# A stated wait of 2.2 ahead of the second lane's Gram products in a hybrid RWKV-7 / S5 layer

## The chip, the cores and the metric

The kernel runs on one core of a Trainium2 chip. The time is the device time of one execution in microseconds (us); lower is better. Before the change three timed executions took 1517.97, 1521.6 and 1523.78 us, so the median is 1521.6 us. The execution that the profiler recorded took 1524.13 us by the same clock; its span, from the first to the last recorded instruction, is 1522.3 us.

The core has a matrix engine (PE, with its weight loads listed as PEld), a vector engine (DVE), an engine for activations and copies (ACT), a general engine (POOL) and a queue engine that only issues transfers (SP). Each runs its own list of instructions in order, and waits at an instruction until what it needs is there. POOL and SP issue the DMA transfers of this kernel. PE writes its results to PSUM, a memory of a few banks, from which DVE or ACT must take them before the bank can be written anew.

## The reference

One decoder layer on `x` of shape (1, 1024, 1024), in float32. Only the part around the change is given in full:

```python
h  = rms_norm(x, norm_mix_pre)
p  = h @ w_in              # RWKV columns | S5 input u | two gates
yA = rwkv7_branch(p_rwkv)  # 8 heads of 64, 1024 time steps
yB = s5_branch(u)          # diagonal complex state space, 64 states per group
m  = sigmoid(gA) * (yA @ wA) + sigmoid(gB) * (yB @ wB)
x  = x + rms_norm(m @ w_out, norm_mix_post)
x  = x + rms_norm(conv_ffn(rms_norm(x, norm_ffn_pre)), norm_ffn_post)

# inside rwkv7_branch, per head (S is 64 x 64)
S = S * w_t + (S @ a_t) b_t^T + v_t k_t^T
y_t = S @ r_t
bonus = sum(r * k * r_k, over the head) * v      # added to y
```

## The kernel before

**Matrix products.** Every large product is computed in three passes from a high and a low part of each operand (lines 180, 181, 182, on 128x512 tiles). A group of these three matmuls is called a *step* here.

**RWKV.** The recurrence is not run step by step. Time is cut into chunks of 64, and within a chunk the products of all pairs of time steps (the *Gram products*) are formed, masked, and a triangular system is inverted. The work is divided into four *pairs* i = 0..3, two groups of heads by two halves of time (512 steps each). Each pair goes through these stages:

1. the *front* (`rwkv_front`), run by two lanes u = 0 and 1, each for half of the group's heads. It ends with two sets of Gram products (line 752, 32 matmuls of 64x128 each, into two PSUM banks), their masked copy to `gr` by DVE (line 754), the transfer of the diagonal blocks to DRAM as `md` (line 760, POOL), and the *bonus sum*: one product with a block matrix of ones (line 763, into one PSUM bank), which DVE multiplies by `v` (line 764), and which is stored as `bv` (line 765).
2. the *inverse* (`rwkv_inv`): 31 steps on DVE (lines 810 and 812) on the blocks of `md`; POOL stores the result to DRAM (line 815) and loads it back into `gr` (line 822, eight transfers).
3. the *level* (`rwkv_level`): two DVE transposes of `gr` (line 835), PE products of 32x32 (line 838), ACT copies of them (line 839), PE products with these (line 840), ACT copies (line 841). It combines the 32-blocks to 64-blocks.
4. the *chain* (`rwkv_chain`, lines 870 to 913) over the chunks, and the output of the pair.

**PSUM.** The Gram products, the bonus sum and a few others draw from one tag `rp` with two banks. A set of Gram products takes both, the bonus sum takes one.

**The order.** On PE the order is that in which the program is written: the whole block runs under a manual schedule for PE. `drive()` writes it. It keeps a clock of its own, `self.now`, and a list of lanes: `chain_lane` first, then `prep_lane(0)` and `prep_lane(1)` (which run the fronts and the inverse of a pair), then a lane for a late product. Each lane is a generator. When it has written a piece it yields the PE time of the piece and a delay (or a condition) until its next piece may stand. The first lane in the list that is ready goes next; when none is ready, or too much of PE's recent time went to lanes, `background()` writes one step of the projections of the gates and of the branches, with a planned PE time of 0.68. A piece that becomes ready later therefore stands behind more such steps; the steps are the same ones, drawn from one list.

Two conditions matter here. Ahead of each set of Gram products a lane waits until `self.now >= self.masked`, and then sets `self.masked = self.now + 1.8 + T_GR` with T_GR = 2.5: the next set, of whichever lane, is not to stand before DVE has emptied the two banks. The bonus sum has no part in this: it neither waits for `masked` nor sets it.

On DVE, ACT, POOL and SP a scheduler orders the instructions by priorities and by its own estimate of when each can run. That order is fixed when the program is built.

**The tail of the program.** Behind the RWKV branch come the merge, the output projection, the norms and the feed-forward part, nearly all of it PE steps.

Of the kernel before, what the change touches and what calls it, by code (L numbers as in the profile page):

```python
# [73 lines left out]
class Kern:  # L74
# [607 lines left out]
    def rwkv_front(self, d, u, i):  # L682
# [81 lines left out]
        V.tensor_tensor(r, pb, v, ALU.mult)  # L764
        nc.gpsimd.dma_start(d["bv"][u], r)
        d["v"][u] = v
        yield 0.55, 1.5

    def rwkv_nat(self, d):
# [1329 lines left out]
T_LD, T_LT = 14.0, 3.0  # L2099
NEVA = 4  # L2100
T_KN, T_BK, T_GR, T_INV, T_LV, T_CH, T_LN, T_LF = 12.0, 10.0, 2.5, 58.0, 1.0, 0.8, 12.0, 12.0
T_X, T_GLU = 3.0, 25.0
T_N0, T_RS, T_N1, T_N2, T_N4, T_N5, T_N3 = 2.5, 4.0, 2.2, 20.0, 1.6, 24.0, 2.0
NET = 5
T_PN = 8.0
# [87 lines left out]
```

## Time and profile before

| | before |
|---|---|
| median of three timed runs | 1521.6 us (1517.97 to 1523.78) |
| the profiled execution, its own time | 1524.13 us |
| its span | 1522.3 us |
| mean granted PE clock | 0.991 of full speed |
| PE busy | 1469.8 us, 97% of the span |
| DVE busy | 1158.5 us, 76% |
| ACT busy | 726.6 us, 48% |
| POOL busy | 180.2 us, 12% |
| the RWKV stage, from the first front's Gram products to the last chain | about 290 to 720 us of the span |

The views used below: the *waits* list, for each engine and line, the time idle ahead of it and what ended the idle time; the *timeline* has one row for each run of equal instructions (start in us, duration of the run in us, engine, line, operation, output<-inputs, count, and in brackets the idle time just before and what ended it); the *windows* give, for a stretch of the span, each engine's busy time with its count of instructions, then the granted PE clock (1.00 is full speed), the busy share of the DMA engines (1.05 means that all of them were taken) and GB/s. Consecutive matmuls overlap: what counts is the distance from one start to the next, not the duration in the row. "A<-B" in brackets reads "until B of that line was done".

### The profile page before, as it was taken

The page shows a single profiled execution, that of the slowest core. Times are in us where ns is not written, and L with a number is a line of the kernel's source. Part 1 is how long each engine was busy: PE and PEld are TensorE (multiplying, and loading weights), DVE is VectorE, ACT ScalarE, POOL GpSimd, SP SyncE. Part 2 cuts the span into 40 slices and gives each one's busy share as a digit, 9 for nine tenths or more (in the row PEclk, how much of TensorE's full clock was granted, in tenths as well). Part 3 has the DMA queues.
Part 4 walks back from the last instruction along what each step waited for, and adds up shares of the span by engine and source line. Part 5 has one row for each costly group of instructions (what it writes and reads, how often), then busy time and mean ns, then how long its engine had stood idle before and what let it go on. Part 6 is the DMA issues. An engine that isn't in the chain of part 4 may idle for free.

```text
span 1522.3 us, 23902 instructions
## 1 busy us (share of the span) xinstructions
PE 1469.8 (97%) x8804; PEld 1166.1 (77%) x8804; DVE 1158.5 (76%) x2157; ACT 726.6 (48%) x1209; POOL 180.2 (12%) x340
## 2 busy tenths in 40 slices
PE   7999999999999998999999999999999999999997
PEld 5788787787677675666788778888888887888875
DVE  7989974765655594975767888888888888698767
ACT  5465444331453434556635555555555555444451
POOL 0022111124021232030110010000000000000000
PEclk9999999999999998999999999999999999999999
DMA  6455344444332446452456575233333336944712
GB/s 211 135 154 159 98 139 145 143 135 152 107 124 96 128 120 192 146 167 70 157 189 199 182 242 180 93 108 117 113 110 117 112 109 225 333 154 138 246 59 111
DMA packets 121558, 225.26 MB, mean 148 GB/s; under 512 B 31024, under 2 KB 37168, under 8 KB 121440
## 3 DMA queue, kind: packets, MB, share of 16 engines
q1 hardware_dynamic: 90576, 154.77, 32.5%
q0 software_dynamic: 21024, 64.71, 12.9%
q10 hardware_dynamic: 9840, 4.24, 1.1%
q8 instruction: 69, 1.13, 0.3%
q14 instruction: 49, 0.40, 0.1%
HBM read 164.16 MB, written 57.41 MB: 146 GB/s over the span
## 4 chain that ended last, share of the span: by engine, by line
PE 44%; DVE 4%; DMA 4%; ACT 1%; issue 1%; SPq 0%; DVEq 0%; ACTq 0%
PE d L1779 8%; PE rp L1600 5%; PE rp L1602 5%; PE rp L1601 5%; PE mm L1602 2%; PE mm L1600 2%; PE mm L1601 2%; DMA st<-in_w_down_dram 2%; PE ch L181 1%; PE mm L180 1%; PE ch L182 1%; PE mm L181 1%; PE gm L180 1%; PE ch L180 1%; PE mm L182 1%
## 5 line engine op out<-in xcount | busy, mean ns | idle before, releaser
L180 PE MATMUL gm<-hh,wh 128*128 128x512 f32 x672 | 283.1, 421 | 1.9 <-DVE ev L1057 1.9
L181 PE MATMUL gm<-hl,wh 128*128 128x512 f32 x672 | 264.9, 394 | 0.1
L182 PE MATMUL gm<-hh,wl 128*128 128x512 f32 x672 | 264.7, 394 | 0.0
L160 ACT CAST wh<-wf 128x512 fp32r<-128x512 f32 x181 | 111.9, 619 | 171.5 <-PE gm L181 88.5
L161 DVE TENSOR_TENSOR wl<-wf,wh 128x512 fp32r<-128x512 f32 x181 | 124.3, 690 | 86.5 <-ACT wh L160 84.5
L180 PEld LDWEIGHTS gm<-hh,wh 128*128 128x128 f32 x672 | 127.0, 189 | 34.3 <-issue 4.0
L182 PEld LDWEIGHTS gm<-hh,wl 128*128 128x128 f32 x672 | 127.0, 189 | 28.1
L181 PEld LDWEIGHTS gm<-hl,wh 128*128 128x128 f32 x672 | 127.4, 190 | 22.5 <-DVE hl L246 1.0
L1779 PE MATMUL d<-xh,wl 128*128 128x512 f32 x308 | 113.5, 392 | 2.1 <-DVE wl L246 2.1
L1779 PE MATMUL d<-xh,wh 128*128 128x512 f32 x308 | 113.9, 393 | 1.1 <-DVE zg L1630 1.1
L1779 PE MATMUL d<-xl,wh 128*128 128x512 f32 x308 | 113.4, 392 | 0.6 <-DVE xl L246 0.6
L1600 PE MATMUL rp<-t,h 128*128 128x512 f32 x252 | 98.3, 390 | 1.4 <-ACT p L1614 1.4
L1602 PE MATMUL rp<-t,l 128*128 128x512 f32 x252 | 98.0, 389 | 0.0
L1601 PE MATMUL rp<-t,h 128*128 128x512 f32 x252 | 98.0, 389 | 0.0
L1779 PEld LDWEIGHTS d<-xh,wl 128*128 128x128 f32 x308 | 58.1, 189 | 15.1 <-DVE wl L246 2.9
L1779 PEld LDWEIGHTS d<-xh,wh 128*128 128x128 f32 x308 | 57.8, 189 | 14.2 <-DVE zg L1630 1.5
L246 DVE TENSOR_TENSOR l<-r,h 128x1024 fp32r<-128x1024 f32 (+1 forms) x40 | 38.9, 971 | 38.9 <-ACT h L245 38.9
L1779 PEld LDWEIGHTS d<-xl,wh 128*128 128x128 f32 x308 | 58.2, 189 | 13.2 <-DVE xl L246 0.9
L245 ACT CAST h<-r 128x1024 fp32r<-128x1024 f32 (+1 forms) x40 | 33.9, 849 | 69.5 <-PE rp L1601 67.2
L1621 DVE SCALAR_TENSOR_TENSOR y<-zv,vecs,y 128x1023 f32<-128x1023 f32 (+1 forms) x42 | 53.7, 1280 | 10.2 <-ACT y L1619 10.2
L1600 PEld LDWEIGHTS rp<-t,h 128*128 128x128 f32 x252 | 47.3, 188 | 11.9 <-ACT p L1614 2.2
L1601 PEld LDWEIGHTS rp<-t,h 128*128 128x128 f32 x252 | 47.3, 188 | 9.8
(476 smaller groups left out, 3338.1 us busy)
## 6 DMA issues: line engine op xcount, KB each, us to landing
r<-in_w_up_dram SPq DMA_DIRECT2D x42, 512.0 KB, 3.5
wf<-in_w_in_dram SPq DMA_DIRECT2D x72, 256.0 KB, 3.1
st<-in_w_down_dram SPq DMA_DIRECT2D x55, 256.0 KB, 4.3
st<-ACT SPq DMA_DIRECT2D x44, 256.0 KB, 4.2
ACT<-y POOLq DMA_DIRECT2D x21, 512.0 KB, 2.9
GT<-ev POOLq DMA_DIRECT2D x32, 256.0 KB, 3.5
wf<-in_w_br_dram SPq DMA_DIRECT2D x32, 256.0 KB, 3.4
wf<-in_w_out_dram SPq DMA_DIRECT2D x32, 256.0 KB, 2.8
```

What stands on the lines that cost most here:

```text
L160: self.last_wh = nc.scalar.copy(h[:, :n], f[:, :n])
L161: low = nc.vector.tensor_tensor(l[:, :n], f[:, :n], h[:, :n].bitcast(F32), ALU.subtract)
L180: mm(ps, a, xh[k], start=a0, stop=False)
L181: mm(ps, a, xl[k], start=False, stop=False)
L182: mm(ps, b, xh[k], start=False, stop=z0)
L245: a = self.nc.scalar.copy(hi, x)
L246: self.split_ops = a, (eng or self.nc.vector).tensor_tensor(lo, x, hi.bitcast(F32), ALU.subtract)
L1600: mm(ps, wh[:, c], xh, start=first and k == 0, stop=False, skip_group_check=True)
L1601: mm(ps, wh[:, c], xl, start=False, stop=False, skip_group_check=True)
L1602: mm(ps, wl[:, c], xh, start=False, stop=k == 3, skip_group_check=True)
L1621: V.scalar_tensor_tensor(y[:, lag:], z[:, 0:1024 - lag], self.vec(nme, i), y[:, lag:], ALU.mult, ALU.add)
L1779: mm(ps, w[:, c], y[:, x], start=start and k == 0, stop=stop and k == 2, skip_group_check=True)
```

## The change

After a lane has written its bonus sum, `masked` is moved to at least `now + 2.2`. The piece that was affected by `masked` before, the next set of Gram products of either lane, now counts the bank of the bonus sum as well.

```diff
         V.tensor_tensor(r, pb, v, ALU.mult)
         nc.gpsimd.dma_start(d["bv"][u], r)
         d["v"][u] = v
+        self.masked = max(self.masked, self.now + T_PB)
         yield 0.55, 1.5
...
-T_X, T_GLU = 3.0, 25.0
+T_X, T_GLU, T_PB = 3.0, 25.0, 2.2
```

The added line shifts the numbers of all lines behind it by one: line 822 of before is 823 after, 835 is 836, 838 is 839, 839 is 840, 840 is 841, 1284 is 1285. Lines 752 to 765 keep their numbers.

No instruction is added or removed. What moves is shown at three places. First PE, in the first pair, at the end of lane 0's front; the rows are matmuls with their output tile and operands (`gm` is the bank that a projection's steps add up in, `hh`, `hl`, `wh`, `wl` the parts of the operands). Before:

```order
L180 MATMUL gm_3021<-hh_853,wh_2853 128x512
L181 MATMUL gm_3021<-hl_854,wh_2853 128x512
L182 MATMUL gm_3021<-hh_853,wl_2854 128x512
L763 MATMUL rp_3038<-ld_2628,csts 128x512
L752 MATMUL rp_3042<-ar_2745,bk_2746 64x128
L752 MATMUL rp_3043<-ar_2745,bk_2746 64x128
```

And in the changed kernel:

```order
L182 MATMUL gm_3021<-hh_853,wl_2854 128x512
L763 MATMUL rp_3038<-ld_2628,csts 128x512
L180 MATMUL gm_3021<-hh_858,wh_2859 128x512
L181 MATMUL gm_3021<-hl_859,wh_2859 128x512
L182 MATMUL gm_3021<-hh_858,wl_2860 128x512
L180 MATMUL gm_3021<-hh_863,wh_2859 128x512
L181 MATMUL gm_3021<-hl_864,wh_2859 128x512
L182 MATMUL gm_3021<-hh_863,wl_2860 128x512
L180 MATMUL gm_3021<-hh_868,wh_2859 128x512
L181 MATMUL gm_3021<-hl_869,wh_2859 128x512
L182 MATMUL gm_3021<-hh_868,wl_2860 128x512
L752 MATMUL rp_3064<-ar_2745,bk_2746 64x128
```

Lane 1's first Gram products stood directly behind lane 0's bonus sum, and now stand behind three more steps. The same is so in pair 1; in pairs 2 and 3 two or three pieces lie between, some of them products of the level (line 838) in place of steps. Everything that the lanes write behind this place stands two to six steps further back among the steps, up to the last chain; behind that the order on PE is the same as before.

Second, DVE, where pair 2 reaches its level while the front of pair 3 ends (`x` and `gr` are the tiles of the level's transpose, and the `gr` written by line 754 is that of pair 3). Before:

```order
L161 TENSOR_TENSOR wl_6352<-wf_6353,wh_6351 128x512
L835 STREAM_TRANSPOSE x_6155<-gr_4616 32x512
L754 TENSOR_TENSOR gr_5718<-rp_6132,csts 128x4x128
L835 STREAM_TRANSPOSE x_6155<-gr_4616 32x512
L754 TENSOR_TENSOR gr_5718<-rp_6133,csts 128x4x128
L161 TENSOR_TENSOR wl_6507<-wf_6508,wh_6506 128x512
L764 TENSOR_TENSOR ld_5728<-rp_6186,ld_6017 128x512
L754 TENSOR_TENSOR gr_5718<-rp_6198,csts 128x4x128
```

And in the changed kernel:

```order
L754 TENSOR_TENSOR gr_5724<-rp_6138,csts 128x4x128
L754 TENSOR_TENSOR gr_5724<-rp_6139,csts 128x4x128
L161 TENSOR_TENSOR wl_6392<-wf_6393,wh_6391 128x512
L764 TENSOR_TENSOR ld_5734<-rp_6192,ld_6023 128x512
L1285 SCALAR_TENSOR_TENSOR hl_6170<-hl_6170,gm_6178 128x512
L161 TENSOR_TENSOR wl_6557<-wf_6558,wh_6556 128x512
L836 STREAM_TRANSPOSE x_6164<-gr_4629 32x512 x2
L754 TENSOR_TENSOR gr_5724<-rp_6242,csts 128x4x128
```

The two transposes stood ahead of the bonus sum's multiplication. They now stand behind it, and behind a row that takes a finished projection from `gm_6178` and one that makes the low part of a weight. On PE the last matmul into `gm_6178` stands directly ahead of the level's first products (line 839).

Third, POOL's queue at the same place. Before:

```order
L815 DMA xd_5512<-x_5413 512x1x32 x4
L1140 DMA GT_90<-ev_6047 128x512
L696 DMA ld_6030<-RKV_102 128x512
L822 DMA gr_4616<-xd_5512 32x8x32 x8
L1140 DMA GT_89<-ev_6093 128x512
L760 DMA md_5720<-gr_5718 32x8x32 x3
L1253 DMA ev_6274<-YU_107 128x512
```

And in the changed kernel:

```order
L816 DMA xd_5540<-x_5441 512x1x32 x4
L760 DMA md_5726<-gr_5724 32x8x32
L823 DMA gr_4629<-xd_5540 32x8x32 x8
L1141 DMA GT_90<-ev_6167 128x512
L1254 DMA ev_6208<-YU_107 128x512
L1254 DMA ev_6215<-YU_108 128x512
```

The eight loads of the inverse of pair 2 into `gr`, which the transposes read, stood ahead of the first store of `md` of pair 3 and now stand behind it.

## The prediction, made before the changed kernel ran

> **What bounds the kernel now.** I read the page's busy times first, then the waits of PE, then the windows and the timeline of the RWKV stage.
>
> ```profile
> span 1522.3 us, 23902 instructions
> ...
> PE 1469.8 (97%) x8804; PEld 1166.1 (77%) x8804; DVE 1158.5 (76%) x2157; ACT 726.6 (48%) x1209; POOL 180.2 (12%) x340
> ```
>
> PE is busy for 1469.8 of 1522.3 us. Only 52.5 us are idle in the whole program, so a change that adds and removes no PE work can win a part of these and no more, apart from what it does to PE's clock. The RWKV stage holds the changed order; its window is this:
>
> ```profile
> 290.00:740.00 450.00, 432.98 (x4046) 316.92 (x4045) 291.88 (x800) 207.45 (x479) 96.40 (x177) 0.98 0.43 129
> ```
>
> PE is idle there for 450.00 - 432.98 = 17.0 us, at a mean clock of 0.98. DVE (291.88) and ACT (207.45) have room. Two lines of PE's waits lie in this stretch and are touched by the change:
>
> ```profile
> PE chk L840 <- ACT x L839: 3.8, 2, 3.4
> PE rp L752 <- DVE ld L764: 2.3, 3, 1.3
> ```
>
> The second is the wait that the change speaks of: Gram products (line 752) for the multiplication (line 764) that frees the bank of the bonus sum. The list gives 2.3 us in 3 waits. The first is the longest wait of the stage, 3.4 us in one piece, in the level of pair 2.
>
> **Term A: the waits that go.** There are four places, the end of lane 0's front in each pair. PE's timeline at the first three:
>
> ```profile
> 299.59 1.02 PE L763 MATMUL rp<-ld,csts 128*128 128x512 f32 x2
> 300.54 0.43 PE L752 MATMUL rp<-ar,bk 64*64 64x128 f32 x2
> 301.55 1.10 PE L752 MATMUL rp<-ar,bk 64*64 64x128 f32 x30 [0.58 <-DVE ld L764]
> ...
> 355.12 1.13 PE L763 MATMUL rp<-ld,csts 128*128 128x512 f32 x2
> 356.17 0.43 PE L752 MATMUL rp<-ar,bk 64*64 64x128 f32 x2
> 357.92 1.10 PE L752 MATMUL rp<-ar,bk 64*64 64x128 f32 x30 [1.32 <-DVE ld L764]
> ...
> 495.22 1.12 PE L763 MATMUL rp<-ld,csts 128*128 128x512 f32 x2
> 496.27 0.43 PE L752 MATMUL rp<-ar,bk 64*64 64x128 f32 x2
> 497.12 1.10 PE L752 MATMUL rp<-ar,bk 64*64 64x128 f32 x30 [0.42 <-DVE ld L764]
> ```
>
> Two Gram matmuls run into the free bank, and the other thirty stand until the second bank is free. And at the fourth place, with an undisturbed set of Gram products for comparison:
>
> ```profile
> 575.15 1.02 PE L763 MATMUL rp<-ld,csts 128*128 128x512 f32 x2
> 576.10 0.44 PE L838 MATMUL chb<-x,gr 32*32 32x32 f32 x16
> 576.47 1.58 PE L752 MATMUL rp<-ar,bk 64*64 64x128 f32 x32
> 577.98 0.50 PE L180 MATMUL gm<-hh,wh 128*128 128x512 f32 x1
> ...
> 581.76 1.10 PE L752 MATMUL rp<-ar,bk 64*64 64x128 f32 x32
> 582.80 0.50 PE L180 MATMUL gm<-hh,wh 128*128 128x512 f32 x1
> ```
>
> Undisturbed, 32 of them take 582.80 - 581.76 = 1.04 us to the next start, so two take 0.07. The four places lose 301.55 - 300.54 - 0.07 = 0.94, 1.75 - 0.07 = 1.68, 0.85 - 0.07 = 0.78, and 577.98 - 576.47 - 1.04 = 0.47. That is **3.9 us**. The bracketed idle times alone (the 2.3 of the list) are the lower bound, since a stopped run of matmuls also loses its overlap.
>
> Do the waits go entirely? In the new order three steps stand between. One step is the distance of two starts:
>
> ```profile
> 584.31 0.39 PE L180 MATMUL gm<-hh,wh 128*128 128x512 f32 x1
> ...
> 585.00 0.40 PE L180 MATMUL gm<-hh,wh 128*128 128x512 f32 x1
> ...
> 585.47 0.39 PE L182 MATMUL gm<-hh,wl 128*128 128x512 f32 x1
> 589.28 0.24 PE L840 MATMUL chk<-gr,x 32*32 32x32 f32 x2 [3.42 <-ACT x L839]
> ```
>
> That is 0.69 us, so Gram starts 0.95 (the bonus sum, 300.54 - 299.59) + 3 x 0.69 = 3.0 us after the bonus sum did. At place 2, the latest, DVE frees the bank here:
>
> ```profile
> 357.19 0.68 DVE L764 TENSOR_TENSOR ld<-rp,ld 128x512 f32<-128x512 f32 x1
> ```
>
> It ends at 357.87, which is 2.75 us after 355.12. The margin is 0.25 us; at places 1 and 3 Gram could go on 1.96 and 1.90 us after the bonus sum's start, so 1 us is left. I take the whole 3.9. The steps that fill the gap are drawn from the same list and would have run later, so they cost nothing in themselves, and all else that moves back among them costs nothing while its consumers have slack. In pairs 0 and 1 the inverse and the level leave it; in pair 2 they do not.
>
> **Term B: what is late next.** In pair 2 the order on DVE and POOL changes so that the level starts late. What it costs today: PE stands 3.42 us at line 840 (3.8 with the second wait of the list), because ACT puts other work ahead of the copies:
>
> ```profile
> 581.66 1.28 ACT L1254 ACT_TABLE_LOAD   x1 [6.03 <-issue]
> ...
> 587.39 0.36 ACT L839 COPY x<-chb 32x256 f32<-32x256 f32 x1
> ```
>
> and behind this stop PE runs at half clock (behind the length of a window stands PE's busy time; the granted clock is the third number from the end):
>
> ```profile
> 575.00:580.00 5.00, 4.95 (x74) 2.97 (x72) 2.67 (x4) 0.63 (x2) 3.25 (x6) 1.00 1.05 387
> ...
> 585.00:590.00 5.00, 1.16 (x8) 0.57 (x8) 4.12 (x6) 4.88 (x10) 1.17 (x3) 0.97 0.36 104
> 590.00:595.00 5.00, 5.00 (x48) 2.62 (x50) 3.45 (x6) 2.94 (x5) 3.04 (x6) 0.50 0.47 127
> 595.00:600.00 5.00, 5.00 (x37) 3.62 (x32) 0.00 (x0) 1.44 (x4) 1.94 (x4) 0.51 0.95 229
> 600.00:605.00 5.00, 4.63 (x54) 3.25 (x53) 1.86 (x4) 1.53 (x5) 0.00 (x0) 1.00 0.49 120
> ```
>
> The loss is 5 x (0.03 + 0.50 + 0.49) = 5.1 us. With the 3.8 of waiting, this place costs **8.9 us** before.
>
> In the changed kernel the first two copies stand ahead of ACT's table load, so the wait at line 840 goes. But a new one stands ahead of the level's first products (838, now 839). They need the two transposes, and these now stand on DVE behind a row (1285) that needs the projection whose last matmul stands directly ahead of 839 on PE, and behind one more row of a weight. So PE waits at least for four DVE rows in line. Each takes about 0.69 as line 764 does: 4 x 0.69 = **2.7 us** as the lower bound. The transposes also need the eight loads of line 823, and these now wait on POOL for the first `md` store:
>
> ```profile
> 565.79 4.64 POOL L822 DMA_DIRECT2D gr<-xd  x8 [1.09 <-DMA xd<-x]
> ...
> 573.42 1.17 POOL L760 DMA_DIRECT2D md<-gr  x2 [2.43 <-DVE gr L754]
> ```
>
> Before, the loads were issued from 565.79, and the first `md` store at 573.42, when Gram of lane 0 had been masked. That event keeps its distance to the bonus sum (575.15). So the loads are issued from 573.42 + 0.58 = 574.0 in steps of 4.64 / 8 = 0.58, the last at 578.06. How long they take to land, here the eight loads of before and then the weights of SP's queue at the same time:
>
> ```profile
> DMA to landing us min/median/max: 3.0/3.5/6.4
> ...
> DMA to landing us min/median/max: 3.4/5.9/8.1
> ```
>
> The last lands at 581.1 to 584.5, by the median at 581.6, and the transposes that stand behind it end 0.7 later. PE is at line 839 one step after the bonus sum, at 575.15 + 0.95 + 0.69 = 576.8. The wait is 581.6 + 0.7 - 576.8 = **5.5 us** by the median and 8.4 by the longest. I take 5.5, the value of the rows nearest to it (the same loads); the DMA share of 1.05 between 575 and 580 says that it can be more. A stop of 5.5 us is longer than the 3.42 that brought half clock before, so I put the same 5.1 us behind it. On ACT, the second pair of copies stands behind the table load and three activations; PE has some 9 us of work before it needs them (five steps, two sets of Gram products, the products of the level), at half clock twice that. I take 0 for a wait there, and 1.2 as the upper end.
>
> Term B: 5.5 + 5.1 - 8.9 = **+1.7 us**.
>
> **The sum.** -3.9 + 1.7 = -2.2 us. Against the profiled execution's own time, 1524.13, this gives 1521.9. The median of the runs is 2.5 lower than that execution (1521.6), so I predict **1519.4 us**.
>
> Bounds of the unknown: the wait at 2.7 and no loss of clock gives 2.7 - 8.9 = -6.2, with term A -10.1, so 1511.5. The wait at 8.4 with 5.1 and 1.2 behind it gives +5.8, with term A +1.9, so 1523.5.
>
> **Rivals.** *The clock comes back sooner* (faster). Half clock does not always last three windows as above. Ahead of this stretch PE had small products of the level between steps, behind it plain steps:
>
> ```profile
> 460.00:463.40 3.40, 3.40 (x10) 2.62 (x9) 3.40 (x15) 0.69 (x1) 0.55 (x1) 0.50 0.16 58
> 463.40:470.00 6.60, 6.24 (x82) 4.13 (x82) 1.46 (x7) 3.50 (x8) 0.00 (x0) 1.00 0.16 52
> ```
>
> Here it lasted 3.4 us, a loss of 1.7. With the new wait of 5.5 and one such stretch, the place costs 7.2 in place of 8.9: -1.7 - 3.9 = -5.6, so 1516.0. With a wait near 2.7, too short to lose the clock, it is the 1511.5 above. For it speaks that the place has fewer 32x32 products behind the stop than before; against it, that they are still mixed with Gram products of 64 rows, while PE was full (5.00 of 5.00) in both slow slices and it did not help.
>
> The Trainium skill, "TensorE: Matmul & The Clock Gate", section "Part 1: The HAM clock gate", states that full rate returns after at least one busy window of about 3.4 us. By this rule the sum would be the 1516.0 of this rival. The trace bears it out at 460, and not at 590 to 600, where 10 us of a full PE passed at half clock; so I weigh the rival at less than half of the forecast.
>
> *The loads of the level land late* (slower). The mechanism is the eight loads in POOL's queue behind the `md` store, in a stretch where the DMA engines are full. If the last takes 8.1 us, as the slowest weight there did, it lands at 586.2, and the wait is 586.2 + 0.7 - 576.8 = 10.1. With half clock one stretch of 3.4 us longer (1.7 more), the place costs 10.1 + 6.8 - 8.9 = +8.0, the whole +4.1, so 1525.7. The point from which it is slower than before: a wait above 8.9 + 3.9 - 5.1 = 7.7 us, that is a landing of the last load more than 5.7 us after its issue. The longest of before, 6.4, is above that; the median of 3.5 is not.
>
> *The change does not do what it says.* Gram waits at the same place for something else, for instance DVE still in the rows of the inverse at place 2, and the level comes out as before. Then the time stays at 1521.6. Against it stands the margin of 1 us at three places.
>
> **How the numbers follow.** Forecast (1511.5 to 1523.5 by its bounds, 1519.4 likeliest) 0.50; clock sooner (1511.5 to 1516.0) 0.22; loads late (1523.5 to 1527) 0.18; nothing 0.10. The range 1511 to 1527 takes all these in. A difference of 0.5%, 7.6 us, is about what a measurement of this kernel can tell from none: faster means below 1514.0, slower above 1529.2. Below 1514.0 lies about half of the second case, 0.10. Above 1529.2 only a wait much longer than the third case comes, or a second loss of clock elsewhere, 0.06. The rest is 0.84.
>
> **What would show it.** No wait of line 752 for line 764 in the waits of PE (term A). A wait of PE at line 839 for DVE's transposes (836) in the level of pair 2, of 2.7 to 8.4 us, with the clock at 0.5 behind it; the wait at line 841, 840 before, gone (term B). A clock that stays at 1.0 there, or a wait above 7.7 us, makes one of the rivals right. PE waits of over 2 us in other pairs would make the prediction wrong, since I take all other shifts as free.

## The result, and the profile after

| | before | changed |
|---|---|---|
| median of eight timed runs of each | 1522.69 us (1517.39 to 1529.79) | 1532.78 us (1530.01 to 1537.55) |
| profiled execution, its own time | 1524.13 us | 1533.01 us |
| its span | 1522.3 us | 1531.2 us |

The ratio is 1.0066, with a 95% interval of 1.0045 to 1.0086: the changed kernel is slower by some 10 us. The forecast was 1519.4 us, its range 1511 to 1527.

The page of the changed kernel, engines:

```profile
span 1531.2 us, 23895 instructions
...
PE 1473.3 (96%) x8804; PEld 1169.6 (76%) x8804; DVE 1159.7 (76%) x2157; ACT 725.9 (47%) x1209; POOL 182.0 (12%) x340
```

PE has the same 8804 matmuls. It is idle for 57.9 us against 52.5, and its busy time has grown by 3.5 us at a mean granted clock of 0.985 against 0.991. The waits of PE, and the window of the RWKV stage with its slow slices (behind the length stands PE's busy time; the clock is the third number from the end):

```profile
PE chk L889 <- DVE S L914: 8.9, 5, 5.8
PE chb L839 <- DVE x L836: 7.1, 2, 6.7
```

```profile
290.00:740.00 450.00, 427.08 (x3986) 313.80 (x3977) 288.24 (x788) 203.24 (x470) 95.85 (x175) 0.97 0.42 127
...
520.00:525.00 5.00, 3.27 (x14) 2.35 (x14) 1.88 (x4) 1.27 (x3) 0.00 (x0) 0.56 0.00 0
525.00:530.00 5.00, 5.00 (x44) 3.73 (x44) 1.27 (x5) 1.56 (x5) 0.71 (x3) 0.76 0.29 105
...
585.00:590.00 5.00, 1.70 (x18) 1.40 (x19) 1.40 (x2) 0.00 (x0) 4.64 (x10) 0.55 0.64 209
590.00:595.00 5.00, 5.00 (x69) 3.51 (x68) 1.29 (x2) 3.51 (x6) 1.06 (x2) 0.50 0.41 130
595.00:600.00 5.00, 5.00 (x57) 3.35 (x55) 2.16 (x3) 3.64 (x5) 0.56 (x1) 0.59 0.21 56
```

The wait of line 752 for line 764 is gone from the list. Two waits of 6 to 7 us have come: one at the level of pair 2 (line 839), which the prediction had, and one in the chain of pair 1 (line 889, 888 before), which it did not. Both bring half clock: the slices hold 5 x (0.44 + 0.24) = 3.4 us and 5 x (0.45 + 0.50 + 0.41) = 6.8 us of lost clock. Not all of it is a loss for PE's work. Windows of half a microsecond show that the clock halves at 520.6 and at 585.5, while PE still stands (until 521.73 and 587.88). Counted from the end of the stop, the half clock costs some 2.9 and 5.6 us.

**What the change was made for happens.** PE's timeline at the first two places:

```profile
298.08 1.02 PE L763 MATMUL rp<-ld,csts 128*128 128x512 f32 x2
...
301.10 1.10 PE L752 MATMUL rp<-ar,bk 64*64 64x128 f32 x32
...
354.81 1.12 PE L763 MATMUL rp<-ld,csts 128*128 128x512 f32 x2
...
357.95 1.10 PE L752 MATMUL rp<-ar,bk 64*64 64x128 f32 x32
```

Gram starts 3.02 and 3.14 us after the bonus sum (3.0 predicted) and runs in one piece of 32. At the third place it is 3.04.

**The new wait in chain 1.** First the changed kernel: PE at the stop, then DVE, then the queue of SP, then the same place in the kernel before (SP's queue, DVE, PE).

```profile
515.56 0.40 PE L182 MATMUL gm<-hh,wl 128*128 128x512 f32 x1
521.73 0.69 PE L889 MATMUL chk<-S,ar 64*64 64x64 f32 x8 [5.77 <-DVE S L914]
```

```profile
512.18 0.28 DVE L903 COPY UV<-chb 64x128 f32<-64x128 f32 x1 [0.85 <-PE chb L900]
520.18 1.23 DVE L718 TENSOR_TENSOR_SCAN ld<-csts,ld 128x512 f32<-128x512 f32 x1 [7.72 <-DMA ld<-TZ]
521.32 0.45 DVE L914 SCALAR_TENSOR_TENSOR S<-chb,pt,spt 128x64 f32<-128x64 f32 x2
```

```profile
510.69 0.39 SPq L696 DMA_DIRECT2D ld<-TZ  x1
```

```profile
511.21 0.38 SPq L696 DMA_DIRECT2D ld<-TZ  x1
```

```profile
518.31 1.23 DVE L718 TENSOR_TENSOR_SCAN ld<-csts,ld 128x512 f32<-128x512 f32 x1 [3.11 <-DMA ld<-TZ]
519.46 0.45 DVE L913 SCALAR_TENSOR_TENSOR S<-chb,pt,spt 128x64 f32<-128x64 f32 x2
```

```profile
519.86 0.45 PE L888 MATMUL chk<-S,ar 64*64 64x64 f32 x8 [0.60 <-DVE S L913]
```

DVE works in order. Ahead of the update of the state S in chunk 6 of chain 1 stands a scan (line 718) of pair 3's front, in both kernels. The scan needs a load into an `ld` tile, and that tile comes free only when lane 1's bonus sum of front 2 has been stored (in the changed kernel the store is issued at 507.90 and lands 2.3 us later; the load goes out at 510.69). Before, 28 matmuls of 128x512 and 80 small ones stood from that bonus sum to the last products of chunk 6, about 7.7 us of PE work at their undisturbed distances, and DVE's wait of 3.1 us cost PE 0.6. The stated wait at front 2 moves lane 1's Gram products and its bonus sum back among the steps, while the chain, first in the list of lanes, keeps its place: 22 and 64 matmuls, about 6.0 us of PE work, are left. The load also took longer: the scan starts 520.18 - 510.69 = 9.5 us after its issue, and 7.1 before. DVE now idles 7.7 us and PE 5.8. PE reaches the stop 3.3 us earlier than before (521.73 - 5.77 = 515.96 against 519.26) and the load goes out only 0.5 us earlier, so 2.8 of the 5.2 us by which PE's wait grew are the shorter distance, and 2.4 are the slower load. In the second profiles (experiment 4) the load took 8.9 us, and again 7.1 in the kernel before. Why it is slower was not tested.

**The level of pair 2.** Its loads go out late, and in this profile not for the reason that the prediction gave. POOL, DVE and PE of the changed kernel:

```profile
577.72 0.59 POOL L760 DMA_DIRECT2D md<-gr  x1 [2.58 <-DVE gr L754]
581.54 4.61 POOL L823 DMA_DIRECT2D gr<-xd  x8 [3.23 <-DMA xd<-x]
```

```profile
587.12 1.43 DVE L836 STREAM_TRANSPOSE x<-gr 32x512 f32<-32x512 f32 x2 [4.17 <-DMA gr<-xd]
```

```profile
587.88 0.31 PE L839 MATMUL chb<-x,gr 32*32 32x32 f32 x2 [6.71 <-DVE x L836]
```

The `md` store was through at 578.31; the loads stood another 3.23 us for the inverse's own store `xd` to land. The inverse itself was late. Here are the windows from its first row on DVE to its last, in the kernel before and then in the changed one (the fourth number is DVE's busy time, with its count):

```profile
527.36:559.40 32.04, 30.72 (x166) 25.64 (x165) 29.98 (x121) 15.13 (x30) 4.11 (x9) 1.00 0.34 105
```

```profile
533.17:570.72 37.55, 36.66 (x192) 30.49 (x191) 35.58 (x124) 17.39 (x32) 5.89 (x12) 1.00 0.35 116
```

It starts 5.8 us later and takes 5.5 us longer. DVE is full in both (29.98 of 32.04, 35.58 of 37.55). The inverse has 62 rows of its own in each; by the program's order 18 full-width rows of other work stand between them before, and 27 in the changed kernel. Five of the nine more belong to the last part of pair 3's front (lines 737 to 741), three make low parts (line 246) and one that of a weight (line 161). At 0.68 to 0.74 us each the nine are some 6.2 us. A third delay stands behind the inverse: from its last row to the loads it is 581.54 - 570.72 = 10.8 us, against 565.79 - 559.40 = 6.4 before, since its stores take longer to land (5.6 us from issue by the median, 2.9 before). PE itself, held in chain 1, comes to the level later too, so these delays do not add up to the wait.

In the second profile of the changed kernel (experiment 4) this wait is less than half as long, and the half clock behind it is one stretch. Its waits, POOL's rows and the windows:

```profile
PE chb L839 <- DVE x L836: 3.0, 2, 2.5
```

```profile
580.19 1.91 POOL L816 DMA_DIRECT2D xd<-x  x3 [1.58 <-issue]
586.23 0.60 POOL L760 DMA_DIRECT2D md<-gr  x1 [4.13 <-DVE gr L754]
586.87 4.61 POOL L823 DMA_DIRECT2D gr<-xd  x8
```

```profile
590.00:595.00 5.00, 2.35 (x25) 1.46 (x27) 2.36 (x4) 0.05 (x1) 3.83 (x8) 0.82 0.58 164
595.00:600.00 5.00, 5.00 (x89) 3.97 (x87) 1.29 (x2) 4.14 (x7) 2.20 (x4) 0.84 0.62 204
```

Here POOL stood 4.13 us ahead of the `md` store and issued the loads directly behind it, as the prediction had it. The inverse was late here too: its last store was issued at 581.42 and took some 4.3 us to land (the median), so that it was through only about 1 us ahead of the loads. The wait of 2.5 us in one piece is near the lower bound of 2.7 that the prediction took from four DVE rows in line. So what the level waits for, and how long, differs between two executions of the same program.

**Where the time went, by stage.** For a sum over all places, each matmul is given the distance to the next start that its shape has in the profile of before where nothing waits. Their sum is PE's work; what a stage takes beyond it is lost time (waits and half clock together). The stages are cut at equal work, with the time at which the kernel before reaches the cut. Both kernels were profiled a second time (experiment 4).

| lost time in us, up to work | 283 us | 489 | 529 | 573 | 608 | 759 | end |
|---|---|---|---|---|---|---|---|
| what stands there | ahead of the change | fronts 0 to 2 | chain 1 | front 3 | level of pair 2 | chain 2, level 3 | the rest |
| before | 18.4 | 36.1 | 10.2 | 3.8 | 15.4 | 30.8 | 21.5 |
| before, second profile | 21.0 | 36.5 | 10.3 | 3.5 | 13.9 | 32.0 | 19.6 |
| changed | 17.5 | 32.8 | 17.5 | 3.1 | 19.0 | 30.6 | 24.8 |
| changed, second profile | 21.9 | 34.7 | 16.2 | 6.4 | 17.3 | 30.8 | 22.4 |

By the means, fronts 0 to 2 give 2.6 us, chain 1 takes 6.6, front 3 takes 1.1 and the level 3.5; the stage behind it gives 0.7. The 3 us of the last column fall almost wholly where the order of all engines is the same in both kernels (from 777 us on).

### The profile page after: what moved, and what is told of

It is laid out like the page before. It is cut to its first block, busy times and chain, and to the rows that moved or that the text cites. A ratio compares the mean times of both kernels' runs of the same rounds, so it can differ in the third digit from the quotient of the medians.

```text
span 1531.2 us, 23895 instructions
## 1 busy us (share of the span) xinstructions
PE 1473.3 (96%) x8804; PEld 1169.6 (76%) x8804; DVE 1159.7 (76%) x2157; ACT 725.9 (47%) x1209; POOL 182.0 (12%) x340
## 4 chain that ended last, share of the span: by engine, by line
PE 73%; DVE 12%; DMA 7%; ACT 3%; issue 3%; POOL 1%; SPq 0%; DVEq 0%; ACTq 0%; POOLq 0%
PE gm L180 9%; PE d L1780 8%; PE gm L181 8%; PE gm L182 8%; PE rp L1601 5%; PE rp L1602 5%; PE rp L1603 5%; PE mm L1602 2%; PE mm L1601 2%; PE mm L1603 2%; DMA st<-in_w_down_dram 2%; DVE wl L161 2%; PE ch L181 1%; PE ch L182 1%; PE ch L180 1%
## 5 line engine op out<-in xcount | busy, mean ns | idle before, releaser
L1622 DVE SCALAR_TENSOR_TENSOR y<-zv,vecs,y 128x1023 f32<-128x1023 f32 (+1 forms) x42 | 53.8, 1280 | 10.2 <-ACT y L1620 10.2
L1601 PEld LDWEIGHTS rp<-t,h 128*128 128x128 f32 x252 | 47.3, 188 | 12.1 <-ACT p L1615 2.2
L1603 PEld LDWEIGHTS rp<-t,l 128*128 128x128 f32 x252 | 47.3, 188 | 9.9
```

The source lines that it names most:

```text
L1601: mm(ps, wh[:, c], xh, start=first and k == 0, stop=False, skip_group_check=True)
L1603: mm(ps, wl[:, c], xh, start=False, stop=k == 3, skip_group_check=True)
L1622: V.scalar_tensor_tensor(y[:, lag:], z[:, 0:1024 - lag], self.vec(nme, i), y[:, lag:], ALU.mult, ALU.add)
```

## The experiments

The kernel before ran beside each of them on the same chip; its median there was 1520.7 us (experiments 1 and 2), 1522.9 (3 and 4), 1523.3 (5) and 1522.7 (6).

**1. Is it the scan?** Theory 1: the late scan in chain 1 makes the loss. Theory 2: the level makes it alone. The order is added to the changed kernel:

```diff
-                V.scalar_tensor_tensor(S[:, u], psn[:, u], ...
+                self.state = V.scalar_tensor_tensor(S[:, u], psn[:, u], ...
...
             self.tc.add_manual_dep(scan.ins, self.levelled.ins.name, ORDER)
+        if i == 3:
+            self.tc.add_manual_dep(scan.ins, self.state.ins.name, ORDER)
```

> The changed kernel, with one order added on DVE: the scans of the last front (line 718) stand behind the last update of the state in the chain of pair 1. Theory 1 (late scan): the 10 us come from the scan, which waits for its load and holds the state update of chunk 6 behind it; so the wait of 5.8 us ahead of line 889 and the half clock behind it (6.8 us long, 3.4 lost) go, the inverse of pair 2 starts some 6 us earlier, the wait at the level of pair 2 falls from 7.1 to under 4, and the time is 1516 to 1523. Theory 2 (level alone): the chain of pair 1 has slack behind the scan, the loss is made at the level of pair 2, by loads that stand behind the md store; so the level still waits about 7 us and the time is 1529 to 1533.

Measured: 1530.01 us (1526.9 to 1532.22), ratio 1.0049 [1.0029, 1.0070]. The wait in the chain is gone, and chain 1 loses 9.2 us, as before the change. But the level waits as long as it did:

```profile
PE chb L841 <- DVE x L838: 7.2, 2, 6.8
```

The inverse of pair 2 started earlier, and took 39.8 us instead: 28 full-width rows stand between its own. So theory 1 was right on the place, while the time and the wait at the level are those that theory 2 gave (1529 to 1533, about 7 us). Theory 2's reason, slack in chain 1, does not hold: chain 1 lost 16.2 to 17.5 us in the changed kernel. The scan is one cause; taken away alone it gives back some 3 of 10 us, and the intervals of the two ratios overlap, so even these 3 are not clear of noise.

**2. Which of the fronts?** The stated wait is set only for some of them.

```diff
-        self.masked = max(self.masked, self.now + T_PB)
+        if i != 2:
+            self.masked = max(self.masked, self.now + T_PB)
```

> The stated wait for fronts 0, 1 and 3 only; front 2 as before. Theory 1: 7.7 us of PE work between lane 1's bonus sum of front 2 and chunk 6 as before, no wait of several us ahead of the chain, 1517 to 1523. Theory 2: front 3 still moves the level's loads and transposes, wait of 5 to 7 us there and half clock behind it, 1527 to 1532.

> The stated wait for front 2 only. Theory 1: PE work between lane 1's bonus sum of front 2 and chunk 6 falls from 7.7 to 6.0 us as in the changed kernel, so the wait ahead of the chain's next products is 4 to 7 us, with half clock behind it; 1526 to 1534. Theory 2: the wait is absorbed, 1519 to 1524.

> The stated wait for front 3 only. Theory 1: nothing ahead of it moves, the wait at the fourth place goes (0.5 us) and little else; 1519 to 1524. Theory 2: the level of pair 2 stands late, 1526 to 1532.

| | median | ratio | PE work from the bonus sum to chunk 6 | inverse of pair 2 |
|---|---|---|---|---|
| fronts 0, 1, 3 | 1535.61 | 1.0088 [1.0066, 1.0110] | 7.7 us | 36.8 us |
| front 2 only | 1533.11 | 1.0073 [1.0045, 1.0100] | 6.0 us | 37.5 us |
| front 3 only | 1526.94 | 1.0029 [1.0010, 1.0047] | 7.7 us | 32.0 us |

The medians of the first two rows are of four runs each. By theory 1 they would have been 1517 to 1523, 1526 to 1534 and 1519 to 1524, by theory 2 1527 to 1532, 1519 to 1524 and 1526 to 1532. Front 2 alone came out as theory 1 has it and front 3 alone as theory 2 has it; fronts 0, 1 and 3 are slower than either gave.

Front 2 alone brings the wait in chain 1 (its line is 890 here) and the late level:

```profile
PE chb L840 <- DVE x L837: 6.1, 2, 5.7
PE chk L890 <- DVE S L915: 4.6, 3, 3.4
```

Fronts 0, 1 and 3 do not bring the wait in the chain, as theory 1 says, and yet the kernel is no faster than with all four (1.0088 against 1.0066, with overlapping intervals). Its waits are spread, the longest at the level:

```profile
PE chb L840 <- DVE x L837: 3.6, 2, 3.2
```

and the inverse of pair 2 is stretched here too. Front 3 alone leaves the inverse as it was, and moves a wait to the level's last step:

```profile
PE chk L842 <- ACT gr L843: 6.7, 2, 6.4
```

No single place carries the loss, and no theory of one place explains the three. What the four slowest kernels so far share (the changed one and those of experiments 1 and 2 without front 3 alone), and the kernel before and front 3 alone do not, is the stretched inverse.

**3. The stretched inverse, alone and with the scan.** Theory 3: nine more full-width rows of front 3 stand between the rows of the inverse. The order is added to the changed kernel:

```diff
+            self.inverted = V.tensor_tensor(x[:, :, 0:ns, q + 1:32], ...
...
-        V.scalar_tensor_tensor(kk, k, self.vec("k_k", p), kb, ...
+        op = V.scalar_tensor_tensor(kk, k, self.vec("k_k", p), kb, ...
+        if i == 3:
+            self.tc.add_manual_dep(op.ins, self.inverted.ins.name, ORDER)
```

> The changed kernel, with one order added on DVE: the last part of pair 3's front (from the row that takes the norm, line 737, to the rows of line 741) stands behind the last step of the inverse of pair 2. Theory 3 (stretched inverse): 27 full-width rows stand between the inverse's 62 in the changed kernel, 18 in the kernel before; at 0.65 us each the nine more are the 5.5 us by which the inverse takes longer (37.5 against 32.0), and the level of pair 2 is late by that. With 19 between them it takes 32 to 33 us, the loads of the level go out ahead of the md stores, the wait at the level falls from 7.1 to under 3 us; the wait in the chain of pair 1 (5.8 us) stays. Time 1523 to 1528. Rival (DVE is full): DVE has no room between 520 and 690 us, and rows that are put back here are late in front 3 or in chain 2; the wait goes to another line and the time stays at 1530 to 1534.

> The changed kernel with both orders: the scans of the last front behind the state of chain 1, and its last part behind the inverse of pair 2. Theories 1 and 3 together: no wait of over 3 us in chain 1 and at the level of pair 2, and the four waits of line 752 stay gone, so the time is below that of the kernel before: 1514 to 1521. Rival (DVE is full): 1526 to 1532 as with the first order alone.

The order alone: 1531.2 us (1526.64 to 1537.34), ratio 1.0053 [1.0030, 1.0077]. The inverse takes 34.5 us, and the wait at the level is gone. The time is the one that the rival of a full DVE gave (1530 to 1534), not that of theory 3 (1523 to 1528). The wait in the chain stays, and front 3 pays a part:

```profile
PE chk L891 <- DVE S L916: 5.3, 2, 4.9
PE rp L754 <- DVE bk L743: 3.5, 2, 2.0
```

Both orders: 1522.24 us (1519.21 to 1526.65), ratio 0.9998 [0.9972, 1.0024]. That is between the two forecasts (1514 to 1521, 1526 to 1532). Each order alone gave back some 3 us, the two together 12 (against 1534.07 of the changed kernel beside it); in the second set of runs (experiment 5) the two together are 1.0028 against 1.0066 and 1.0076 of the changed kernel, which is 6 to 7 us. The level of pair 2 hangs on the inverse, and this on two things, its start and its length; each order mends one:

| pair 2, us | loads of the inverse to its first row | first row to last | loads to the level's first product on PE |
|---|---|---|---|
| before | 16.5 | 32.0 | 65.2 |
| changed | 22.9 | 37.5 | 77.6 |
| scan behind the state | 14.9 | 39.8 | 70.9 |
| rows behind the inverse | 21.4 | 34.5 | 73.9 |
| both | 15.0 | 33.7 | 68.0 |
| before, second profile | 16.5 | 32.1 | 65.0 |
| changed, second profile | 21.5 | 39.3 | 75.3 |
| both, second profile | 15.0 | 34.8 | 68.9 |

(The time of the loads is the issue of the last of the four.)

**4. The same two kernels again**, for the spread of a profile.

> The kernel before, once more, to see how far two profiles of the same kernel differ by stage. If the losses behind 740 us, where the order of all engines is the same in both kernels, are chance (windows at half clock of 3.4 us that fall here or there), this profile differs from the first one by up to 3 us in them; the waits of 1 us and more in the RWKV stage stand at the same lines. All theories: 1518 to 1524.

> The changed kernel, once more, for the same purpose. Theory 1: the load of the scan lands late again, and the wait ahead of line 889 is 4 to 7 us again. If its landing (9.4 us in the first profile) was chance, the wait is under 2 us and the level alone is late. Time 1530 to 1536.

Before 1520.95 us (ratio 0.9988 [0.9963, 1.0012]), changed 1534.07 us (1.0076 [1.0055, 1.0097]). The second profile of before loses 96.2 us in the RWKV stage (283 to 759 us) and the first 96.3; the changed kernel 105.4 and 103.0. The wait for the scan was there again:

```profile
PE chk L889 <- DVE S L914: 8.3, 5, 5.1
```

So it is no accident of one transfer. The wait at the level did not return at its size: it was 3.0 us, as shown above. Ahead of the change, where nothing differs, two profiles of one kernel differ by up to 4.4 us; so the 3 us of the last column of the table are not told from chance.

**5. What is the stated wait worth without its two losses?**

> The kernel before with the two added orders and without the stated wait: what the orders do by themselves. The inverse of pair 2 has 17 full-width rows between its own here (18 before) and the scans now stand behind the state of chain 1, which took 0.6 us of a wait there. If the orders only undo what the change moved, the time is that of the kernel before, 1519 to 1524. If they are a gain of their own (level or chain), it is under 1517, and the return of the changed kernel with them to 1522 is not a repair of its two losses.

> The changed kernel with both orders, once more, to set beside the kernel before with them: the difference of the two is what the stated wait is worth when its two losses are taken away. By the sum of the prediction it is 3.9 us (four waits of line 752), so 1517 to 1520 against 1521 to 1524. If the stage is bound by DVE's chain from front 2 over the inverse of pair 2 to front 3, the gain is taken back by a wait of front 3's Gram products (3 us in the first profile) and the two are equal within 2 us.

> The stated wait for fronts 0 and 1 only, with both orders. Places 1 and 2 keep their gain (2.6 us by the prediction's rows), the two behind them their waits (1.2 us). 20 full-width rows stand in the inverse of pair 2 (19 with all four places). Theories 1 and 3: near both orders with all places, 1518 to 1524. If moving front 2 and 3 is what costs the rest, it is 2 to 4 us faster than that.

The kernel before with both orders: 1522.96 us, ratio 1.0000 [0.9982, 1.0018]. The orders are no gain of their own. The changed kernel with them: 1527.35 us, 1.0028 [1.0008, 1.0048]; this is 5 us above the first time, and both stand. Neither forecast had it: 1517 to 1520, or within 2 us of the kernel before with the orders. Fronts 0 and 1 only, with both orders: 1525.0 us, 1.0007 [0.9993, 1.0022], a little above the 1518 to 1524 that theories 1 and 3 gave. So with its two losses taken away the stated wait is worth between nothing and a small loss, and not the 3.9 us of term A. Lost time shows where it goes:

| | fronts 0 to 2 | chain 1 | front 3 | level of pair 2 | chain 2, level 3 |
|---|---|---|---|---|---|
| before, mean of two | 36.3 | 10.3 | 3.7 | 14.7 | 31.4 |
| changed, both orders | 32.1 | 9.2 | 8.4 | 8.0 | 35.6 |
| the same again | 34.9 | 9.2 | 9.5 | 7.8 | 35.5 |

PE comes to front 3 earlier and waits there for DVE. PE and the windows in the first of the two profiles:

```profile
566.17 0.40 PE L756 MATMUL rp<-ar,bk 64*64 64x128 f32 x2 [2.08 <-DVE bk L745]
```

```profile
565.00:570.00 5.00, 2.93 (x34) 2.32 (x35) 3.43 (x6) 0.00 (x0) 0.97 (x2) 0.70 1.01 307
570.00:575.00 5.00, 5.00 (x36) 3.78 (x38) 1.46 (x3) 0.62 (x1) 4.69 (x9) 0.62 1.02 309
```

The inverse and the rows that now follow it hold DVE until then; PE has gained time and spends it there, at 0.70 and 0.62 of its clock.

**6. Is the level's price of 8.9 us there to be had?** The kernel before, without the stated wait; the activations that bring a new table stand behind the four copies of the level.

```diff
+    def hold_gelu(self, d, copy):
+        if d is self.ds[2]:
+            for y in self.gelus:
+                self.tc.add_manual_dep(y.ins, copy.ins.name, ORDER)
...
```

> The kernel before, without the stated wait, with one order added on ACT: the activations that bring in a new table (line 1254 of before) stand behind the four copies of the level of pair 2 (line 839). This takes the largest wait of the RWKV stage by itself, and measures the 8.9 us that the prediction puts on this place (3.8 of waiting, 5.1 of half clock). If that price is right and nothing behind the activations is late, the wait ahead of line 840 goes, PE keeps its clock there, and the time is 1512 to 1517, faster than both kernels. If the glu products behind the activations wait instead, or DVE's chain takes it back as it does with both orders, it is 1518 to 1524.

Measured: 1526.9 us (1522.42 to 1531.41), ratio 1.0030 [1.0012, 1.0047], above both forecasts (1512 to 1517, 1518 to 1524). The wait at the level's products left the copies of one line for those of the next:

```profile
PE chk L845 <- ACT gr L846: 5.8, 3, 3.9
```

and the work behind (chain 2 to level 3) lost 39.6 us in place of 31.4. The half clock at this place fell to one stretch:

```profile
590.00:595.00 5.00, 3.04 (x37) 2.10 (x38) 3.76 (x6) 4.08 (x7) 2.39 (x6) 0.75 0.48 161
595.00:600.00 5.00, 4.46 (x38) 3.27 (x37) 1.82 (x4) 1.99 (x6) 1.57 (x3) 0.91 0.92 216
```

The slices lose 5 x (0.25 + 0.09) = 1.7 us, against 5.1 in the first profile of before and 3.4 in the second, and still the time did not fall. None of the versions beats the kernel before clear of noise.

## Why the prediction was wrong, step by step

- **What bounds the kernel.** Right: no more than some us could be won, since PE is busy for 97%. What the prediction did not draw from it is that DVE is full in parts of the stage (29.98 of 32.04 us during the inverse), so that time won by PE there ends in a wait for DVE.
- **Term A, -3.9 us.** The waits went as predicted, with a Gram start 3.02 to 3.14 us after the bonus sum. The lost time of fronts 0 to 2 fell by 3.5 and 1.6 us against a mean of 36.3; the first three places were priced at 3.4.
- **"All else that moves back among them costs nothing while its consumers have slack"**: this is the step that failed. The prediction looked for slack at the inverse and the level, and found it in pairs 0 and 1. It did not look at what is *freed* by the moved work. Lane 1's bonus sum frees the tile of the scan's load, and on DVE the scan stands ahead of chain 1's state. In before, the row was there to be read: DVE's scan with 3.11 us of waiting, and PE's 0.60 behind it, so 0.6 us past its slack already. Chain 1 lost 6.6 us more. Of the 5.2 us that its wait grew by, 2.8 are the moved work and 2.4 a slower load, whose cause stays open.
- **Term B, +1.7 us.** Its sign and place were right, its size was not stable. The wait was 7.1 us in one profile and 3.0 in the other (5.5 predicted, 2.7 to 8.4 as bounds), and the half clock behind it cost 5.6 and 1.7 (5.1 predicted). By lost time the level took 3.5 us more. The cause given holds in the second profile, where the loads went out directly behind the `md` store, though it held them up by only about 1 us. In the first they stood for the inverse's stores instead: the inverse began 5.8 us later than before, took 5.5 us longer, and its stores landed 4.4 us later behind it. The prediction took the inverse as on time. The two orders on DVE remove the wait at the level; most of its price is then paid at front 3 and in chain 2.
- **The rivals.** The slower one came nearest: a wait at the level close to its 7.7 us in the first profile. But its loads were issued late and not slow to land, and at 1525.7 us it was 7 us short, since it had no second place. Of the faster one, half clock for one stretch of 3.4 us came at the level in the second profile, behind a wait of 3.0 us, against 13.7 us in the first; the kernel was no faster for it, since chain 1 waited in both. Its other condition, that a wait near 2.7 us is too short to lose the clock, did not come: the 3.0 us lost it.
- **The range**, 1511 to 1527, was made of bounds on two terms. The term that was taken as nothing had no bound, though the text called a wait of over 2 us elsewhere fatal.

What stays open: why fronts 0, 1 and 3 are as slow as all four; their profile has the stretched inverse, but not a wait as long as the others'. Why the scan's load and the inverse's stores took longer in the changed kernel. And why the changed kernel with both orders took 1522.2 us in one set of runs and 1527.4 in the other.

## What to carry to other kernels

When work is moved behind a stated wait, list what the moved instructions release (tiles, banks, transfers), and for each find the row on an in-order engine that waits for it, and what stands behind that row. A row that already waits a few us in the profile of before, ahead of a chain's own row, is the first to look at: its slack is spent. And where an engine beside the bound one is full for 30 us on end, look whether time won by the bound engine in front of that stretch is kept behind it: here it was not.

## What the runs showed of the hardware

Half clock came in stretches of about 3.4 us, and their number was not fixed by the length of the stop: 3.4 us of idle PE brought 10.2 us of it in one profile of the kernel before, and 3.3 us brought 6.8 in the other at the same place; 5.8 us of idle brought 6.8, and 6.7 us brought 13.7, of which the first 1.1 and 2.4 us fell into the stop itself. In the slices quoted above PE was full (5.00 of 5.00) at a clock of 0.50. A wait of 2.1 us, with 0.9 more right behind it, was enough for two stretches in the changed kernel with both orders; 2.5 us, with 0.5 more, brought one at the level in the second profile of the changed kernel. The Trainium skill, "TensorE: Matmul & The Clock Gate", section "Part 1: The HAM clock gate", says that full rate returns after at least one busy window of about 3.4 us; these runs show one to four stretches of half clock.
